# Sums laid along the partitions by one product of ones, with a longer start and a vector load in smaller pieces

## The chip, the cores and the metric

The kernel runs on one core of a Trainium2 chip. Its metric is the device time of one execution in microseconds (us); the time before is the median of 3 runs, 627.53 us.

## The reference

It is one layer of a hybrid encoder: 512 tokens of 2048 features, all in float32. Attention heads and a linear recurrence work side by side on one shared input projection, and one output projection joins them.

```python
h = rms_norm(x, norm_w)                       # (1, 512, 2048)
proj = einsum('bsd,de->bse', h, w_in)         # 4608 columns
q, k, v, g_attn, xr, g_lru = split(proj, ...) # 1024, 256, 256, 1024, 1024, 1024
attn_out = attention_group(q, k, v, ...)      # 8 heads of 128, 2 of k and v; RMS norm of
                                              # q and k per head, axial rope, full softmax
lru_out = lru_group(xr, conv_w, conv_b, ...)  # depthwise convolution of 4 taps, then a gated
                                              # linear recurrence forward and one backward
mixed = concatenate([rms_norm(attn_out, attn_norm_w) * silu(g_attn),
                     rms_norm(lru_out, lru_norm_w) * silu(g_lru)])
return x + einsum('bse,ed->bsd', mixed, w_out)
```

rms_norm divides each token's vector by the root of the mean of its squares. There are three such norms over whole vectors of features: of x, of lru_out and of attn_out. The change touches how the three sums reach the other partitions.

## The kernel before, in words

The layout is mostly features on the 128 partitions and the 512 tokens along the columns. A float32 product is split: each operand becomes a high part in fp32r and a low part (the rest, in fp32r too), and mm3 adds three matmuls in PSUM, high by high, high by low, low by high (L153 to L155). The high part of a weight tile is a cast on ScalarE (L218, wh from the raw weights wr), the low part a subtraction on VectorE (L219, wl). A weight transfer brings 256 input features by 512 columns; a projection takes 8 of them. The output projection is done in 2x2 blocks with seven products in place of eight (L1029).

The order on TensorE is the order of the code throughout, under manual_schedule. On SP, the queue of most transfers, it is written by hand in the start and in the attention, on ScalarE and VectorE in the start and at the end. Elsewhere a scheduler orders the instructions of VectorE, ScalarE and GpSimd, and brings marked ones forward (high_priority). Chains of small work (the recurrence, the norms, the attention) are woven into projections: the chain yields a number, and so many steps of the projection are issued before it goes on.

The parts that the change touches stand in this order in the program:

- **The start.** GpSimd sets constants: ident (an identity, L159), ones (L161), ones_r (a copy of ones in fp32r), nhalf. TensorE begins with WARM = 11 products of ones, the fillers of busy() (L1156), while the first chunk of x and nw_st (the norm's gains) are on their way. Then columns() transposes nw_st (L189), xturn() transposes the first x (L253), ScalarE writes its high part, WARM2 = 5 more fillers run, and the first projection begins (L388).
- **vec_load() (L170)** fetches seven kinds of small vectors (convolution taps conv_w, biases, decay parameters, norm gains) into vec_st, a row of 128 numbers each, in seven transfers on SP's queue. columns(vec, vec_st) then transposes it on TensorE (L189), and the copy (L191) makes vec, in which each vector is a column.
- **rows() (L352)** takes rstd, the 1/rms of x, in which a token is a partition, and has to lay it along the columns, the same on all partitions, as rbc. It splits rstd into a high and a low part, multiplies each with the identity (L360: a diagonal block for each 128 tokens), and adds two products of ones with these diagonals in one PSUM bank (L367). rbc scales the evacuation of each projection (L471).
- **halved() and spread() (L817, L825)** serve the other two norms. The squares are added over the tiles into sums["l"] (hsum, L568 on VectorE and L570 on GpSimd) and sums["a"] (asum, L751 on GpSimd), a column for each token, with 128 partial sums down the partitions. halved() makes a high and a low part of the sum (L821, L822), spread() two products of ones with them (L829), which add up the partitions and leave the total on each, then the square root and the reciprocal, into gbc. kv() calls them for the recurrence beside the attention's q projection, later() for the attention beside the last gate projection.

The calls that a reader needs beside the functions below:

```python
    busy(WARM)
...
        if (c, e) == (4, 2):
            with tc.high_priority(AHEAD):
                vec_load()
        if (c, e) == (7, 1):
            columns(vec, vec_st)
        if (c, e) in ((4, 3), (KT // 2 - 1, 0)):
            with tc.high_priority(AHEAD), tc.issue_after(split_done[-1][1]):
                next(stats)
```

Of the kernel before, what the change touches and what calls it, by code (L numbers as in the profile page):

```python
# [12 lines left out]
F32R = mybir.dt.float32r  # L13
# [4 lines left out]
P = 128  # L18
# [3 lines left out]
NT = SEQ // P  # L22
# [4 lines left out]
NB = 8  # L27
# [12 lines left out]
SOON = 150  # L40


WARM, WARM2 = 11, 5


BEGIN, STEPS, LATE = 11, 2, 3
# [13 lines left out]
R_CW, R_CB, R_BA, R_BX, R_LAM, R_AN, R_LN, R_END = 0, 32, 40, 56, 72, 88, 96, 104  # L60
# [3 lines left out]
def hybrid_kernel(  # L64
# [20 lines left out]
    nc = tc.nc  # L85
# [32 lines left out]
    def nm(s):  # L118
        cnt[0] += 1
        return f"{s}_{cnt[0]}"  # L120
# [22 lines left out]
    def mm():  # L143
        return ps.tile([P, SEQ], F32, tag="mm", name=nm("mm"))

    def const(shape, name, dt=F32):
        return cp.tile(list(shape), dt, tag=name, name=name)

    def f(ap):
        return ap.bitcast(F32)  # L150
# [4 lines left out]
        nc.tensor.matmul(acc, ll, rh, start=False, stop=stop)  # L155


    ident = const([P, P], "ident")
    make_identity(nc, ident)  # L159
    ones = const([P, P], "ones")  # L160
    nc.gpsimd.memset(ones, 1.0)  # L161
    ones_r = const([P, P], "ones_r", F32R)
    nc.gpsimd.memset(f(ones_r), 1.0)
    nhalf = const([P, 48], "nhalf")
    nc.gpsimd.memset(nhalf, -0.5)

    nw_st = const([KT, P], "nw_st")
    vec_st = const([R_END, P], "vec_st")

    def vec_load():  # L170
        for lo, src in (
            (R_CW, conv_w.rearrange("t o (n p) -> (t o n) p", p=P)),
            (R_CB, conv_b.rearrange("(n p) -> n p", p=P)),
            (R_BA, lru_ba.rearrange("d (n p) -> (d n) p", p=P)),
            (R_BX, lru_bx.rearrange("d (n p) -> (d n) p", p=P)),
            (R_LAM, lru_lambda.rearrange("d (n p) -> (d n) p", p=P)),
            (R_AN, attn_norm_w.rearrange("(n p) -> n p", p=P)),
            (R_LN, lru_norm_w.rearrange("(n p) -> n p", p=P)),
        ):
            nc.sync.dma_start(vec_st[lo : lo + src.shape[0], :], src)  # L180
# [62 lines left out]
    def behind(those):  # L243
        stack = ExitStack()
        for ins in those:
            stack.enter_context(tc.issue_after(ins))
        return stack
# [103 lines left out]

    def rows(dst, col, dg):  # L352

        shape = [P, NT, P]
        part = [const([P, NT], nm("part")) for _ in range(2)]
        parts = [dg() for _ in part]
        nc.vector.tensor_copy(part[0].bitcast(F32R), col)
        nc.vector.tensor_sub(part[1], col, part[0])
        for c, d in zip(part, parts):
            nc.vector.tensor_mul(  # L360
                d, ident[:, None, :].broadcast_to(shape), c[:, :, None].broadcast_to(shape)
            )
        yield
        pb = mm()
        for k, d in enumerate(parts):
            d = d.rearrange("p t q -> p (t q)")
            nc.tensor.matmul(pb, ones_r, d, start=k == 0, stop=k == 1)  # L367
        nc.vector.tensor_copy(dst, pb)
        yield

    def xstats():
        s = const([P, NT], "xsum")
        nc.vector.reduce_sum(s, ssq, axis=AX.X)
        rsqrt_mean(rstd, s, DM, NT)
        yield from rows(rbc, rstd, lambda: k2(F32R, (P, NT, P)))
# [278 lines left out]
    def kv(es):  # L654
        turned_k = sent(norm_rope(es, NKV, rk), NKV)
        yield 20
        opened("wx", "right")
        for t in range(NT):
            vv = es[t][:, NKV * HD :]
            vt = pools["qkv"].tile([P, 2, NKV * HD], F32R, tag="v", bufs=NT, name=nm("v"))  # L660
            vh[t], vl[t] = vt[:, 0, :], vt[:, 1, :]
            nc.scalar.copy(vh[t], vv)
            nc.vector.tensor_sub(vl[t], vv, f(vh[t]))
        yield from lru_squares()
        yield 2
        drain(turned_k)
        yield 6
        pair = landed(asides.pop(0))
        for h in range(NKV):
            yield (12, 4)[h]  # L670
            kt = pools["qkv"].tile([P, 2, SEQ], F32R, tag="kt", bufs=NKV, name=nm("kt"))
            kth[h], ktl[h] = kt[:, 0, :], kt[:, 1, :]
            those = split_head(pair, h, kth[h], ktl[h])
        parts = halved(
            sums["l"],
            lambda: pools["rope"].tile([P, SEQ], F32R, tag="kv", bufs=NT, name=nm("kv")),
            those,
        )
        yield 4
        spread(gbc, parts, NB * P)  # L680
# [135 lines left out]

    def halved(src, tile_of, those=()):  # L817

        hi, lo = tile_of(), tile_of()
        with behind(those):  # L820
            nc.scalar.copy(hi, src)  # L821
            nc.vector.tensor_sub(lo, src, f(hi))  # L822
        return hi, lo

    def spread(dst, parts, n, those=()):  # L825

        pb = mm()
        for k, part in enumerate(parts):
            nc.tensor.matmul(pb, ones_r, part, start=k == 0, stop=k == 1)  # L829
        nc.scalar.activation(dst, pb, AF.Sqrt, scale=1.0 / n, bias=eps[:, :1])  # L830
        for t in range(NT):
            ts_ = slice(t * P, (t + 1) * P)
            with behind(those):
                nc.vector.reciprocal(dst[:, ts_], dst[:, ts_])
# [122 lines left out]
    own = []  # L957
# [254 lines left out]
    for step in proj_feat(C_XR, a1, first, given):  # L1212
        if step is None:
            with tc.high_priority():
                first.append(wsplit(raw, 1, nc.vector.tensor_copy))
                xturn(xc, 1)
            xsquare(xc, 0)
            move(None)
            given[1] = wload(w_in, 2 * P, C_XR)
            continue  # L1220
        c, e = step
        move(step)
        if (c, e) == (1, 2):
            s2.close()
# [8 lines that stand above are left out]
# [121 lines left out]
    def later():  # L1354
        with tc.high_priority():
            parts = halved(sums["a"], lambda: fin_s(dt=F32R))
        yield 2
        with tc.high_priority():
            spread(gbc, parts, NH * HD, split_done[turn_of[0] - 2][1:])
        yield 4  # L1360
        for pair in ap_[:2]:
            normed(pair)
        yield 4
        todo = gate(late, ap_[:2], R_AN, fin_s)
        for _ in range(3):
            yield next(todo)
        build(4, ap_[0], [hring.tile([P, 7, H], F32R, name=nm(t)) for t in ("mh", "ml")])
        yield from todo
        for pair in ap_[2:]:
            normed(pair)  # L1370
# [78 lines left out]
```

## Time and profile before

| what | value |
|---|---|
| median of 3 runs | 627.53 us (627.31 to 627.67) |
| span of the profiled execution | 625.3 us (the page gives no other time of that execution) |
| TensorE busy | 620.3 us, 99% of the span, 2758 matmuls |
| TensorE weight loads (beside the matmuls) | 512.8 us, 82% |
| VectorE busy | 494.8 us, 79% |
| ScalarE busy | 353.2 us, 56% |
| GpSimd busy | 101.7 us, 16% |
| DMA | 127.61 MB, mean 204 GB/s |

The profile comes from one execution, and its span runs from the first to the last recorded instruction. In its rows, PE is TensorE, PEld its weight loads, DVE VectorE, ACT ScalarE, POOL GpSimd, SP the engine whose queue issues most transfers; SPq and the like are the queues. L360 is line 360 of the kernel before, and "k<-ident,part" reads: tile k written from ident and part, buffer numbers left out. A matmul's "busy" time overlaps the next one's, so the pace of TensorE is read from the distance of starts, not from its busy share or from the mean of one.

### The profile page before, as it was taken

The numbers are of one execution on the slowest core, as the hardware profiler recorded it, in microseconds if no ns is written. First come the engines' busy times: TensorE is split into PE (matmuls) and PEld (weight loads), VectorE is DVE, ScalarE is ACT, GpSimd is POOL, SyncE is SP. The second block draws the span as 40 slices with busy tenths as digits, with TensorE's granted clock in tenths as the row PEclk, the third lists the DMA queues.
The fourth block names the chain that finished last, engine by engine and source line by source line (L and its number), as shares of the span: only waits on it lengthen the run. The fifth ranks groups of instructions, "written<-read, shape, count | busy, mean of one in ns | idle before, by whom it ended". The sixth has DMA issues, their size and how long they took to land.

```text
span 625.3 us, 8281 instructions
## 1 busy us (share of the span) xinstructions
PE 620.3 (99%) x2758; PEld 512.8 (82%) x2758; DVE 494.8 (79%) x796; ACT 353.2 (56%) x617; POOL 101.7 (16%) x134
## 2 busy tenths in 40 slices
PE   9999999999999999999999999999999999999997
PEld 7888888888888888888888888888888888888886
DVE  5967979986699875987887888549979866886886
ACT  3764899479945823545485448428445633443441
POOL 0000210112003531622123223100310101010010
PEclk9999999999999999999999999999999999999999
DMA  8878785859774599479658646923995677896262
GB/s 289 293 210 253 179 206 163 175 136 197 236 231 140 169 235 250 103 204 273 186 175 258 201 140 192 265 79 106 261 248 185 210 253 240 293 327 233 68 202 101
DMA packets 73595, 127.61 MB, mean 204 GB/s; under 512 B 6617, under 2 KB 29265, under 8 KB 73553
## 3 DMA queue, kind: packets, MB, share of 16 engines
q1 hardware_dynamic: 65664, 109.65, 56.7%
q0 software_dynamic: 7712, 17.31, 14.3%
q8 instruction: 21, 0.34, 0.2%
q14 instruction: 22, 0.17, 0.1%
q10 hardware_dynamic: 176, 0.14, 0.1%
HBM read 110.29 MB, written 37.75 MB: 237 GB/s over the span
## 4 chain that ended last, share of the span: by engine, by line
PE 99%; DVE 0%; issue 0%; POOL 0%; POOLq 0%
PE pj L153 20%; PE pj L154 20%; PE pj L155 20%; PE mm L1029 14%; PE pj L1029 11%; PE mm L155 3%; PE mm L154 3%; PE mm L153 3%; PE pj L388 2%; PE mm L253 1%; PE mm L1156 1%; PE mm L829 0%; PE mm L367 0%; DVE cb L1058 0%; PE mm L189 0%
## 5 line engine op out<-in xcount | busy, mean ns | idle before, releaser
L153 PE MATMUL pj<-x,wh 128*128 128x512 f32 x368 | 143.5, 390 | 0.0
L155 PE MATMUL pj<-x,wl 128*128 128x512 f32 x368 | 143.2, 389 | 0.0
L154 PE MATMUL pj<-x,wh 128*128 128x512 f32 x368 | 143.2, 389 | 0.0
L218 ACT CAST wh<-wr 128x512 fp32r<-128x512 f32 x142 | 84.9, 620 | 78.9 <-PE pj L154 31.2
L219 DVE TENSOR_TENSOR wl<-wr,wh 128x512 fp32r<-128x512 f32 x144 | 99.9, 724 | 19.7 <-ACT wh L218 18.6
L881 ACT CAST wh<-wr 128x1024 fp32r<-128x1024 f32 (+1 forms) x72 | 60.8, 862 | 75.7 <-PE mm L1029 34.6
L882 DVE TENSOR_TENSOR wl<-wr,wh 128x1024 fp32r<-128x1024 f32 (+1 forms) x72 | 68.8, 985 | 30.5 <-ACT wh L881 30.3
L155 PEld LDWEIGHTS pj<-x,wl 128*128 128x128 f32 x368 | 69.1, 188 | 14.5
L153 PEld LDWEIGHTS pj<-x,wh 128*128 128x128 f32 x368 | 69.1, 188 | 14.3
L154 PEld LDWEIGHTS pj<-x,wh 128*128 128x128 f32 x368 | 69.1, 188 | 14.3
L153 PE MATMUL pj<-wh,x 128*128 128x512 f32 x192 | 74.7, 389 | 0.0
L155 PE MATMUL pj<-wh,x 128*128 128x512 f32 x192 | 74.7, 389 | 0.0
L154 PE MATMUL pj<-wl,x 128*128 128x512 f32 x192 | 74.7, 389 | 0.0
L905 POOL DMA_DIRECT2D t<-in_w_out_dram x40 | 33.5, 891 | 156.6 <-DMA t<-in_w_out_dram 99.4
L1029 PE MATMUL mm<-wh,ml 128*128 128x512 f32 x126 | 49.0, 389 | 0.0
L1029 PE MATMUL mm<-wh,mh 128*128 128x512 f32 x126 | 49.0, 389 | 0.0
L1029 PE MATMUL mm<-wl,mh 128*128 128x512 f32 x126 | 49.0, 389 | 0.0
L155 PEld LDWEIGHTS pj<-wh,x 128*128 128x128 f32 x192 | 36.0, 188 | 7.6
L153 PEld LDWEIGHTS pj<-wh,x 128*128 128x128 f32 x192 | 36.0, 188 | 7.5
L154 PEld LDWEIGHTS pj<-wl,x 128*128 128x128 f32 x192 | 36.0, 188 | 7.4
L706 POOL TENSOR_SCALAR p<-p,sm 128x512 f32<-128x512 f32 x32 | 24.3, 762 | 89.4 <-DVE sm L705 89.4
L1029 PE MATMUL pj<-wl,mh 128*128 128x512 f32 (+1 forms) x100 | 38.5, 385 | 0.0
(201 smaller groups left out, 1053.6 us busy)
## 6 DMA issues: line engine op xcount, KB each, us to landing
wr<-in_w_in_dram SPq DMA_DIRECT2D x71, 512.0 KB, 5.1
wr<-in_w_out_dram SPq DMA_DIRECT2D x24, 512.0 KB, 5.1
t<-in_w_out_dram POOLq DMA_DIRECT2D x40, 256.0 KB, 6.9
wr<-t SPq DMA_DIRECT2D x40, 256.0 KB, 5.4
pd<-u SPq DMA_DIRECT2D x16, 512.0 KB, 3.0
pt<-pd SPq DMA_DIRECT2D x64, 128.0 KB, 3.6
t<-in_w_out_dram SPq DMA_DIRECT2D x24, 256.0 KB, 5.4
t<-t SPq DMA_DIRECT2D x16, 256.0 KB, 5.1
```

Source lines behind the costliest of these rows:

```text
L153: nc.tensor.matmul(acc, lh, rh, start=start, stop=False)
L154: nc.tensor.matmul(acc, lh, rl, start=False, stop=False)
L155: nc.tensor.matmul(acc, ll, rh, start=False, stop=stop)
L218: copy(hi, raw[:, k, :]).ins,
L219: nc.vector.tensor_sub(lo, raw[:, k, :], f(hi)).ins,
L253: nc.tensor.transpose(pt[:, t * P : (t + 1) * P], xc[:, t, ks], ident)
L388: nc.tensor.matmul(acc[e], w[:, e * P : (e + 1) * P], x_[2 * c + k], start=c == k == j == 0, stop=False,)
L706: last_pool[0] = nc.gpsimd.tensor_scalar(p, p, sm, 0.0, op0=ALU.mult, op1=ALU.add).ins
L881: nc.scalar.copy(hi[:, to], b)
L882: nc.vector.tensor_sub(lo[:, to], b, f(hi[:, to]))
L905: nc.gpsimd.dma_start(dst, src, accum_op=ALU.add)
L1029: nc.tensor.matmul(dst[s][:, es], lh[:, ts_], rh[:, es], start=i == ends_[0] and j == 0, stop=i == ends_[1] and j == 2,)
```

## The change

Four edits:

- **One product.** rows() puts the high part of a token's value into one half of the partitions and the low part into the other half: "two" holds both, and both_ is a matrix that carries the 64x64 identity in each of its four quarters, so that each column of the operand d has two nonzero entries, the high part and the low part. One product of ones adds them. halved() first adds the upper 64 partitions of the sum to the lower 64 (on VectorE, in place), then writes the high part of those 64 into the lower half of one tile and the low part into the upper half; spread() does one product.
- **The constants.** VectorE sets ones, as its first instruction, and GpSimd has one memset less; GpSimd makes both_ from ident with an addition and a copy, after ident and nhalf.
- **The fillers.** WARM is 12 in place of 11.
- **The loads.** vec_load() fetches the four convolution taps in four transfers of 8 rows each in place of one of 32 rows.

```diff
--- before.py
+++ after.py
@@ -40,7 +40,7 @@
 SOON = 150
 
 
-WARM, WARM2 = 11, 5
+WARM, WARM2 = 12, 5
 
 
 BEGIN, STEPS, LATE = 11, 2, 3
@@ -155,21 +155,29 @@
         nc.tensor.matmul(acc, ll, rh, start=False, stop=stop)
 
 
+    ones = const([P, P], "ones")
+    nc.vector.memset(ones, 1.0)
     ident = const([P, P], "ident")
     make_identity(nc, ident)
-    ones = const([P, P], "ones")
-    nc.gpsimd.memset(ones, 1.0)
     ones_r = const([P, P], "ones_r", F32R)
     nc.gpsimd.memset(f(ones_r), 1.0)
     nhalf = const([P, 48], "nhalf")
     nc.gpsimd.memset(nhalf, -0.5)
 
+    both_ = const([P, P], "both")
+    half = P // 2
+    nc.gpsimd.tensor_add(both_[:, :half], ident[:, :half], ident[:, half:])
+    nc.gpsimd.tensor_copy(both_[:, half:], both_[:, :half])
+
     nw_st = const([KT, P], "nw_st")
     vec_st = const([R_END, P], "vec_st")
 
     def vec_load():
         for lo, src in (
-            (R_CW, conv_w.rearrange("t o (n p) -> (t o n) p", p=P)),
+            *(
+                (R_CW + t * NB, conv_w[t].rearrange("o (n p) -> (o n) p", p=P))
+                for t in range(R_CB // NB)
+            ),
             (R_CB, conv_b.rearrange("(n p) -> n p", p=P)),
             (R_BA, lru_ba.rearrange("d (n p) -> (d n) p", p=P)),
             (R_BX, lru_bx.rearrange("d (n p) -> (d n) p", p=P)),
@@ -351,20 +359,21 @@
 
     def rows(dst, col, dg):
 
-        shape = [P, NT, P]
-        part = [const([P, NT], nm("part")) for _ in range(2)]
-        parts = [dg() for _ in part]
-        nc.vector.tensor_copy(part[0].bitcast(F32R), col)
-        nc.vector.tensor_sub(part[1], col, part[0])
-        for c, d in zip(part, parts):
-            nc.vector.tensor_mul(
-                d, ident[:, None, :].broadcast_to(shape), c[:, :, None].broadcast_to(shape)
-            )
+        shape = [P, NT, 2, P // 2]
+        two = const([P, NT, 2], "two", F32R)
+        for n in range(2):
+            own, other = (slice(m * P // 2, (m + 1) * P // 2) for m in (n, 1 - n))
+            nc.vector.tensor_copy(two[own, :, n], col[own])
+            nc.vector.tensor_sub(two[other, :, n], col[own], f(two[own, :, n]))
+        d = dg()
+        nc.vector.tensor_mul(
+            d.rearrange("p t (h q) -> p t h q", h=2),
+            both_.rearrange("p (h q) -> p h q", h=2)[:, None].broadcast_to(shape),
+            f(two)[:, :, :, None].broadcast_to(shape),
+        )
         yield
         pb = mm()
-        for k, d in enumerate(parts):
-            d = d.rearrange("p t q -> p (t q)")
-            nc.tensor.matmul(pb, ones_r, d, start=k == 0, stop=k == 1)
+        nc.tensor.matmul(pb, ones_r, d.rearrange("p t q -> p (t q)"), start=True, stop=True)
         nc.vector.tensor_copy(dst, pb)
         yield
 
@@ -816,17 +825,18 @@
 
     def halved(src, tile_of, those=()):
 
-        hi, lo = tile_of(), tile_of()
+        both = tile_of()
+        low, high = src[: P // 2], src[P // 2 :]
+        nc.vector.tensor_add(low, low, high)
         with behind(those):
-            nc.scalar.copy(hi, src)
-            nc.vector.tensor_sub(lo, src, f(hi))
-        return hi, lo
-
-    def spread(dst, parts, n, those=()):
+            nc.scalar.copy(both[: P // 2], low)
+            nc.vector.tensor_sub(both[P // 2 :], low, f(both[: P // 2]))
+        return both
+
+    def spread(dst, both, n, those=()):
 
         pb = mm()
-        for k, part in enumerate(parts):
-            nc.tensor.matmul(pb, ones_r, part, start=k == 0, stop=k == 1)
+        nc.tensor.matmul(pb, ones_r, both, start=True, stop=True)
         nc.scalar.activation(dst, pb, AF.Sqrt, scale=1.0 / n, bias=eps[:, :1])
         for t in range(NT):
             ts_ = slice(t * P, (t + 1) * P)
```

The lines after rows() are 9 further down in the changed kernel's own numbering (L471 is L480 there, L568 is L577), and L219 is L227, L180 is L188. Where the scheduler sets the order, it comes out in another way at some places. Three of them follow.

On VectorE near 50 us of the profile, where the first projection ends: rbc is copied, vec is copied, the first banks are evacuated (ev), and the low parts wl of the next projection's weights are made. Before:

```order
L368 COPY rbc<-mm_626 128x512
L219 TENSOR_TENSOR wl_737<-wr_734,wh_736 128x512
L219 TENSOR_TENSOR wl_741<-wr_734,wh_740 128x512
L500 TENSOR_TENSOR k_121_705<-k_112_684,k_120_704 128x512
L191 COPY vec<-mm_636 128x104
L471 TENSOR_TENSOR ev_696<-pj_161,rbc 128x512
L471 TENSOR_TENSOR ev_698<-pj_162,rbc 128x512
L471 TENSOR_TENSOR ev_700<-pj_163,rbc 128x512
```

Now:

```order
L377 COPY rbc<-mm_632 128x512
L480 TENSOR_TENSOR ev_701<-pj_165,rbc 128x512
L480 TENSOR_TENSOR ev_703<-pj_166,rbc 128x512
L199 COPY vec<-mm_641 128x104
L227 TENSOR_TENSOR wl_742<-wr_739,wh_741 128x512
L227 TENSOR_TENSOR wl_746<-wr_739,wh_745 128x512
L480 TENSOR_TENSOR ev_705<-pj_167,rbc 128x512
L509 TENSOR_TENSOR k_118_710<-k_109_689,k_117_709 128x512
```

Two evacuations and the copy of vec moved ahead of the two low parts.

On SP's queue, near the end of the first projection, stand the loads of the small vectors and behind them the weights of the next projection (wr) and the recurrence's gate maps (k). Before:

```order
L180 DMA vec_st<-in_conv_w_dram 32x128
L180 DMA vec_st<-in_conv_b_dram 8x128
L180 DMA vec_st<-in_lru_ba_dram 16x128
L180 DMA vec_st<-in_lru_bx_dram 16x128
L180 DMA vec_st<-in_lru_lambda_dram 16x128
L180 DMA vec_st<-in_attn_norm_w_dram 8x128
L180 DMA vec_st<-in_lru_norm_w_dram 8x128
L206 DMA wr_734<-in_w_in_dram 128x2x512
```

Now four loads of conv_w stand in place of the first row, and everything behind them is three places further back; the prediction shows the rows.

On VectorE near 205 us, in kv(), where the recurrence's squares are added up and the sum is handed to halved(). Before:

```order
L281 STREAM_TRANSPOSE uq_2057<-kv_1680 128x2x4x32
L568 TENSOR_TENSOR hsum<-hsum,hsq_2039 128x1024
L219 TENSOR_TENSOR wl_2273<-wr_2270,wh_2272 128x512
L219 TENSOR_TENSOR wl_2277<-wr_2270,wh_2276 128x512
L613 TENSOR_TENSOR ev_2100<-ev_2100,rr_2108 128x512
```

The rows of now are in the prediction: the addition of the two halves (64x512) stands between L568 and the two low parts, and so a wait for GpSimd's L570 does too.

## The prediction

> **What bounds the kernel now.** I read the page's first section, then TensorE's waits, then its chain, then the chip's time in three stretches.
>
> ```profile
> span 625.3 us, 8281 instructions
> PE 620.3 (99%) x2758; PEld 512.8 (82%) x2758; DVE 494.8 (79%) x796; ACT 353.2 (56%) x617; POOL 101.7 (16%) x134
> PE mm L1156 <- POOL ones L161: 1.1, 1, 1.1
> 5.70:621.40 615.70, 615.70 (x2739) 1.00 0.72 205
> ...
> 621.40:625.30 3.90, 0.03 (x1) 0.00 (x0) 0.42 (x1) 0.00 (x0) 0.00 (x0) 0.81 0.40 134
> ```
>
> A busy share of 99% alone would not prove a bound, since matmuls overlap. But the only wait that the list of TensorE's waits shows is the first 1.1 us, for the tile of ones. From 5.70 to 621.40 it is busy for all 615.70 us, and the last 3.90 us are the end of the output. The chain of waits says how fast it goes in between; its columns are start, duration, what.
>
> ```profile
> 1.13 2.53 PE mm L1156 x11
> 3.66 0.21 PE mm L189
> 3.87 1.05 PE mm L253 x4
> 4.92 1.07 PE mm L1156 x5
> 5.98 1.02 PE pj L388 x4
> 7.00 0.44 PE mm L253 x4
> 7.44 3.20 PE pj L388 x14
> ...
> 49.70 0.46 PE mm L367 x2
> ...
> 236.69 0.46 PE mm L829 x2
> ...
> 427.74 0.46 PE mm L829 x2
> ```
>
> Matmuls of 512 columns follow each other every 0.23 us (3.20 / 14), and the products with ones, L367 and L829, go at just that pace: 0.46 us a pair. So the time is the start (6 us), TensorE's list of matmuls at 0.23 us, and the tail. A matmul fewer is worth 0.23 us for certain, unless it opens a wait; a change on another engine is worth nothing until it makes TensorE wait.
>
> The page gives the span of 625.3 us and no time of that execution; the median of the runs, 627.53, is 2.2 us more, and I take those 2.2 us as unchanged. What one run can differ by is seen in 627.31 to 627.67.
>
> **One product of ones in place of two.** Three pairs become single products: 3 x 0.46 / 2 = 0.69 us off TensorE's list. That is the largest term. What replaces them lies on VectorE, ScalarE and GpSimd, and must be ready in time:
>
> ```profile
> L360 DVE TENSOR_TENSOR k<-ident,part x2: 683/684/684, 36.5 to 37.1; 128x512 fp32r<-128x512 f32 x2
> L357 DVE CAST part<-rstd x1: 171/171/171, 36.3 to 36.3; 128x4 fp32r<-128x4 f32 x1
> L568 DVE TENSOR_TENSOR hsum<-hsum,hsq x3: 1186/1187/1222, 198.8 to 204.0; 128x1024 f32<-128x1024 f32 x3
> L570 POOL TENSOR_TENSOR hsum<-hsum x1: 1621/1621/1621, 205.3 to 205.3; 128x512 f32<-128x512 f32 x1
> L822 DVE TENSOR_TENSOR kv<-hsum,kv x1: 693/693/693, 227.2 to 227.2; 128x512 fp32r<-128x512 f32 x1
> L751 POOL TENSOR_TENSOR asum<-asum,p x7: 1289/1295/1822, 322.6 to 420.0; 128x512 f32<-128x512 f32 x7
> L822 DVE TENSOR_TENSOR s<-asum,s x1: 676/676/676, 422.4 to 422.4; 128x512 fp32r<-128x512 f32 x1
> ```
>
> In rows(), one multiplication of 0.68 us goes and two small instructions come (0.17 each, as L357): the operand is ready at about 37.5 instead of 37.8, and TensorE takes it at 49.7. Nothing there. In halved(), an addition of 64x512 comes ahead of the cast. Its nearest row is L822's 0.69 us (as many columns, half the partitions; below it lies nothing cheaper of that width). The first halved() has its parts at 227.9, and they are read at 236.7: 8.8 us of cover. The second has them at 422.4 + 0.68 = 423.1, read at 427.7: 4.6 us of cover against 0.7, and against about 1.7 more for two casts of hs that ScalarE now does ahead. Cost 0; if the cover were gone, the cost would be what exceeds it.
>
> The first new addition waits on GpSimd's L570, and it stands right behind the last L568 in VectorE's queue:
>
> ```order
> L577 TENSOR_TENSOR hsum<-hsum,hsq_2044 128x1024
> L830 TENSOR_TENSOR hsum<-hsum 64x512
> L227 TENSOR_TENSOR wl_2278<-wr_2275,wh_2277 128x512
> L227 TENSOR_TENSOR wl_2282<-wr_2275,wh_2281 128x512
> L622 TENSOR_TENSOR ev_2105<-ev_2105,rr_2113 128x512
> ```
>
> So VectorE stands still from 205.2 to 206.9, and the two low parts wl of weights behind it come later. What the same stretch holds today:
>
> ```profile
> 205.07 2.39 DVE L219 TENSOR_TENSOR wl<-wr,wh 128x512 fp32r<-128x512 f32 x2
> 209.07 0.69 DVE L613 TENSOR_TENSOR ev<-ev,rr 128x512 f32<-128x512 f32 x1 [1.62 <-POOL rr L347]
> ...
> 216.68 1.29 DVE L219 TENSOR_TENSOR wl<-wr,wh 128x512 fp32r<-128x512 f32 x2
> ```
>
> The pair took 2.39 us beside GpSimd's L570 and takes 1.29 without it. New: addition 206.9 to 207.6, pair to 208.9, and then L613, which waits for GpSimd until 209.07 anyway. The stall of 1.7 us fits into the gap of 1.62 us and the faster pair. Cost 0.
>
> **Ones set by VectorE, and a twelfth filler.** The fillers L1156 multiply the ones while the first x is on its way.
>
> ```profile
> 0.72 0.20 POOL masks.py:197 MEMSET ident<- 128x128 f32 x1 [0.29 <-POOLq L1434]
> 0.86 0.21 POOL L161 MEMSET ones<- 128x128 f32 x1
> L191 DVE COPY nw<-mm x1: 175/175/175, 3.9 to 3.9; 128x16 f32<-128x16 f32 x1
> 52.60 0.26 DVE L191 COPY vec<-mm 128x104 f32<-128x104 f32 x1
> ```
>
> Today ones end at 1.07 and TensorE begins at 1.13. No row shows VectorE's memset; between its copies of 16 and of 104 columns it is 0.17 to 0.26 us, from 0.72 as the other engines: ones at 0.89 to 0.98, TensorE at 0.95 to 1.04, that is 0.09 to 0.18 earlier. A filler costs 1.07 / 5 = 0.21. So the fillers end 0.03 to 0.12 later, and L189, the transposes L253, ScalarE's x and the first L388 follow. I take +0.07. The lower bound is 0 (the transposes would wait for x's transfer anyway), the upper one +0.33 (the memset starts only after GpSimd's, 0.93, takes 0.26: TensorE at 1.25, and the filler on top).
>
> The pair above is the row for that upper bound: VectorE and GpSimd slow each other when both work on SBUF. The Trainium skill, "SBUF — State Buffer", section "Who interferes with whom", says that one of the two fully blocks while the other holds a shared port pair, for some of VectorE's kinds of instruction; the trace agrees for L219 (2.39 against 1.29), and no run here shows a memset. [...]
>
> GpSimd's two added instructions make both_ by 2.5 us or so, and it is read at 37.
>
> **Taps one by one.** One transfer becomes four on SP's queue, ahead of the weights of the next product:
>
> ```order
> L188 DMA vec_st<-in_conv_w_dram 8x128 x4
> L188 DMA vec_st<-in_conv_b_dram 8x128
> L188 DMA vec_st<-in_lru_ba_dram 16x128
> L188 DMA vec_st<-in_lru_bx_dram 16x128
> L188 DMA vec_st<-in_lru_lambda_dram 16x128
> L188 DMA vec_st<-in_attn_norm_w_dram 8x128
> L188 DMA vec_st<-in_lru_norm_w_dram 8x128
> L214 DMA wr_739<-in_w_in_dram 128x2x512
> ```
>
> Behind vec_st's loads, three issues more: the weights wr and the gate maps move back.
>
> ```profile
> 41.93 0.32 SPq L180 DMA_DIRECT2D vec_st<-in_attn_norm_w_dram  x1
> 42.59 0.28 SPq L180 DMA_DIRECT2D vec_st<-in_lru_norm_w_dram  x1
> 42.97 0.40 SPq L206 DMA_DIRECT2D wr<-in_w_in_dram  x1
> DMA to landing us min/median/max: 2.1/3.6/5.5
> 47.47 1.30 ACT L218 CAST wh<-wr 128x512 fp32r<-128x512 f32 x2 [1.06 <-PE pj L154]
> 50.80 1.28 DVE L219 TENSOR_TENSOR wl<-wr,wh 128x512 fp32r<-128x512 f32 x2
> 54.26 0.39 PE L153 MATMUL pj<-x,wh 128*128 128x512 f32 x1
> 51.38 0.25 PE L189 MATMUL mm<-ident,vec_st 104*128 104x104 f32 x1
> ```
>
> Each issue takes 0.3 to 0.4 us: +1.0 us or so. The high parts of wr are then ready at 49.8 and read at 54.3. The low parts wait for VectorE, which now puts two evacuations ahead of them, +1.2 us: ready at about 53.3, read at 54.7. The last of vec_st has landed by 42.6 + 5.5 = 48.1 at the latest, by 49.1 with the change, and the transpose L189 reads it at 51.4. Cost 0 in all three, with 1.4 us as the smallest cover.
>
> Sum: 625.3 - 0.69 + 0.07 = 624.7 for the span, 627.53 - 0.62 = 626.9 us for the median.
>
> **Rivals.** (a) The saving is given back: TensorE, 0.23 to 0.69 us ahead, meets producers that do not move with it. For it: VectorE is 79% busy. Against it: the list of waits has nothing for TensorE after 1.1 us, and the producers' own waits are mostly for TensorE, so that they come forward too. Price: the 0.69, 627.5 to 627.9 with the start's upper bound.
>
> (b) The array reaches its full pace sooner. In the chain 256-column fillers need 0.21 and four L388 1.02, where later four need 0.91; the transposes need 1.05 a four and later 0.44. Were all of it at full pace, 0.11 + 0.61 = 0.72 us would go: 626.1 to 626.8. For it: TensorE begins 0.1 us earlier and idles less. Against it: what follows the transposes waits for ScalarE and for weights. The Trainium skill, "TensorE: Matmul & The Clock Gate", Part 1, says that a free-running window of about 3.4 us decides; by that rule an earlier start moves the mean by only a part of the 0.1 us, and one look cannot show it.
>
> (c) The end on the other side: the taps' loads do not overlap. If each of the three waits for the landing of another (2.1 to 5.5 us), vec_st is complete 6.3 to 16.5 us later, up to 48.1 + 16.5 = 64.6, and TensorE stands at L189 from 51.4 on. It decides from 3.3 us of delay, turns the whole slower at 3.9, and is over 0.2% at 5.2: with 8 us it is 627.5 - 0.6 + 4.7 = 631.6. Against it: seven issues went out within 5.4 us while each took 2.1 to 5.5 us to land, so they do overlap.
>
> **How the numbers follow.** 0.2% is 1.25 us, about what a measurement of this kernel can tell from no change. The forecast (626.8 to 627.2 by the start's bounds) has 0.68, (a) 0.14, (b) 0.08, (c) 0.05; 0.05 is left for waits at other places, since the scheduler also reordered VectorE's and ScalarE's work from 50 to 75 and from 420 to 460 us. All but (c), the far end of (b) and that rest lie within 0.2%: faster 0.07, same 0.86, slower 0.07. The range is 626.2 to 627.9: from (b) to (a) with the start's upper bound.
>
> **What would show it.** TensorE with 2756 matmuls, one product each at the lines of the pairs, first start at 0.95 to 1.04, first L388 product between 0 and 0.33 later, no new wait in its list, and a span of 624.6 to 625.0. I am wrong if TensorE's list of waits has an entry beyond its start, above all near 51, 207 or 425 us, or if the first product is more than 0.33 us away from where it is.

## The result, and the profile after

The changed kernel takes 632.29 us (median of 4 runs, 631.73 to 633.39) against 627.42 (4 runs, 627.22 to 627.67): the ratio is 1.0079, 95% interval 1.0065 to 1.0092. It is slower by 4.9 us, where 626.9 was forecast. The profiled execution has a span of 631.2 us. From its page:

```profile
span 631.2 us, 8286 instructions
PE 626.3 (99%) x2756; PEld 512.9 (81%) x2756; DVE 496.3 (79%) x800; ACT 352.4 (56%) x617; POOL 101.7 (16%) x135
```

TensorE has the 2756 matmuls that were forecast and is busy for 6 us more. Its waits (line waited for, us in total, times, longest; behind halved() the changed kernel's lines are 10 further down, not 9, so that L1166 is L1156 of the kernel before):

```profile
PE mm L1166 <- DVE ones L159: 1.0, 1, 1.0
PE pj L155 <- DVE wl L227: 0.2, 1, 0.2
```

So hardly a microsecond of the 5.9 is a wait. The rest has to be the matmuls themselves, and busy time doesn't tell how many fit into a stretch. The table by stretch does: its columns are the stretch, its length and TensorE's busy time in it with the number of matmuls, the granted clock, the DMA share and GB/s. First the kernel before, then the changed one:

```profile
100.00:190.00 90.00, 90.00 (x399) 1.00 0.73 188
190.00:265.00 75.00, 75.00 (x332) 1.00 0.72 183
270.00:420.00 150.00, 150.00 (x663) 1.00 0.68 200
432.00:465.00 33.00, 33.00 (x147) 1.00 0.92 230
470.00:615.00 145.00, 145.00 (x641) 1.00 0.65 214
```

```profile
100.00:190.00 90.00, 90.00 (x397) 1.00 0.72 187
190.00:265.00 75.00, 75.00 (x327) 1.00 0.69 174
270.00:420.00 150.00, 150.00 (x658) 1.00 0.70 203
432.00:465.00 33.00, 33.00 (x147) 1.00 0.83 214
470.00:615.00 145.00, 145.00 (x630) 1.00 0.68 221
```

Every stretch is busy throughout and the granted clock is 1.00, but in 470 to 615 us 630 matmuls are done where 641 were: 230 ns for one instead of 226. From 190 to 265 five are missing, from 432 to 465 none. From start to start, nearly all matmuls of 512 columns of the kernel before are 226 or 227 ns apart. In the changed kernel some 1030 are 229 ns or more apart, most of them 230 to 236; before there are some 75. Summed over all distances below 245 ns, the excess over 226.7 ns is 5.95 us, against 0.35 before. That is +5.6 of the +5.9.

What do the slow ones have in common? Not the engines beside them: from 191 to 254 us they are slow whether VectorE, ScalarE and the DMAs are busy or not (the mean distance is 231.5 ns while VectorE is busy and 230.8 while it is idle). What they have in common is the places of their operands. The constants are laid out one behind the other, and the tiles of the left side (raw weights, x, weights of the projections, later the output's operands) begin behind them. both_ added 512 bytes in each partition. rows() now has one tile "two" of 32 bytes; before it had two tiles "part" of 16 bytes, each rounded up to 32. So everything on the left moved by 512 - 32 = 480 bytes. The tiles of the right side (the recurrence's, q, k, v, the attention's, the first half of the output's operands) stayed. Starts in a partition, modulo 256 bytes, as the program allocates them:

```
kernel            left tiles   right tiles
before               192          192
changed              160          192
```

The slow matmuls stand where one of the operands is from the left and the other from the right (456 matmuls, which lose 2.8 us), or next to a change from one pair of places to another. There they lose 3.1 us although their own two operands are at equal places, all of it in the last matmul before such a change and the next eight behind it. The 1140 that are equal and farther away lose nothing.

From 191 to 254 us the weights of the q projection lie in buffers of the left (xw) and of the right side (wx) in turn, beside x on the left; from 432 to 465 all operands are on the left, and nothing is slow.

What else there is, the chain of the changed kernel shows. Its start:

```profile
1.04 2.74 PE mm L1166 x12
3.79 0.21 PE mm L197
4.00 1.05 PE mm L261 x4
5.04 1.07 PE mm L1166 x5
6.11 1.41 PE pj L397 x4
7.52 0.44 PE mm L261 x4
```

The first product L397 begins at 6.11 instead of 5.98: +0.13, as forecast (between 0 and 0.33). These four need 1.41 instead of 1.02, because TensorE comes to its full pace later in this execution: the first three start distances are 593, 426 and 285 ns, in the kernel before 456, 224 and 231. And at 43 us:

```profile
34.61 3.82 DMA xu<-xd
38.44 3.93 DMA vec_st<-in_conv_w_dram
42.37 0.58 DVE x L347
...
43.59 0.69 DVE wl L227
44.32 0.50 PE pj L155
```

Rows of x that travel through DRAM (xu) come late, ScalarE's and VectorE's work on them does too, the low part wl behind it in VectorE's queue as well, and TensorE's starts are 0.84 us further apart in all around here. Sum: 5.6 + 0.5 + 0.8 - 0.7 for the three products = 6.2 us on TensorE; the tail behind its last matmul is 0.3 shorter.

This execution took 633.39 us, the longest of the four and 1.1 us above their median. The median's +4.9 is just the 5.6 of the pace less the 0.7 of the products. So most of the start's 0.5 and the 0.8 at 43 us are probably this execution's own; there is no second profile of the changed kernel that could show it.

### The profile page after: what moved, and what is told of

Same layout as the page of the kernel before. It is cut to its first block, busy times and chain, and to the rows that moved or that the text cites. A ratio compares the mean times of both kernels' runs of the same rounds, so it can differ in the third digit from the quotient of the medians.

```text
span 631.2 us, 8286 instructions
## 1 busy us (share of the span) xinstructions
PE 626.3 (99%) x2756; PEld 512.9 (81%) x2756; DVE 496.3 (79%) x800; ACT 352.4 (56%) x617; POOL 101.7 (16%) x135
## 4 chain that ended last, share of the span: by engine, by line
PE 96%; DMA 2%; DVE 1%; issue 0%; SPq 0%
PE pj L155 19%; PE pj L153 19%; PE pj L154 19%; PE mm L1039 14%; PE pj L1039 11%; PE mm L155 4%; PE mm L153 3%; PE mm L154 3%; PE pj L397 2%; DMA xd<-xu 1%; PE mm L261 1%; DMA vec_st<-in_conv_w_dram 1%; DMA xu<-xd 1%; PE mm L1166 1%; DVE wl L227 0%; DVE x L269 0%
## 5 line engine op out<-in xcount | busy, mean ns | idle before, releaser
L227 DVE TENSOR_TENSOR wl<-wr,wh 128x512 fp32r<-128x512 f32 x144 | 98.7, 713 | 21.5 <-ACT wh L226 20.4
L1039 PE MATMUL pj<-wh,mh 128*128 128x512 f32 (+1 forms) x100 | 39.0, 390 | 0.0
L1039 PE MATMUL pj<-wh,ml 128*128 128x512 f32 (+1 forms) x100 | 38.9, 389 | 0.0
```

Of the source, the lines that this page charges most:

```text
L227: nc.vector.tensor_sub(lo, raw[:, k, :], f(hi)).ins,
L1039: nc.tensor.matmul(dst[s][:, es], lh[:, ts_], rh[:, es], start=i == ends_[0] and j == 0, stop=i == ends_[1] and j == 2,)
```

## The experiments

Theory 1: TensorE is slowed where the two operands that it reads at once, moving data and weights, start at different places modulo some power of two (64 bytes, I thought at first). Theory 2: the moved instructions, loads and waits make it slow. The first seven kernels move tiles and nothing else; each engine's instructions keep the order that they have in the kernel that was edited. An unused tile of so many bytes behind the constants does it for the left side:

```diff
     nc.gpsimd.memset(eps, EPS)
+    const([P, 8], "gap")           # 8 x 4 = 32 bytes; 16 and 32 for 64 and 128 bytes
```

**The changed kernel, left tiles back to 192.**

> The changed kernel with 32 unused bytes a partition allocated behind its constants, the order of the instructions unchanged. In its profile TensorE's matmuls of 512 columns start 226.7 ns apart where both operands lie at the same offset in 64 bytes, and some 233 ns apart where one tile starts at a multiple of 64 bytes and the other 32 bytes behind one; the slow ones add up to 5.8 us. The constants became 480 bytes longer (512 for both_, less 32 for one tile 'two' in place of two of 'part'), so all tiles of the left side moved by 32 modulo 64. Theory 1 (offset between the operands): the pad takes the offset away; 626.5 to 627.5 us. Theory 2 (the moved instructions, waits and loads make it slow): 631.5 to 633 us, as without the pad.

Measured: 626.77 us (11 runs, 626.14 to 627.66), against 627.29 for the kernel before on the same chip; ratio 0.9991 (0.9982 to 1.0000). 32 unused bytes take away 5.5 us, and what is left is the forecast's time, 626.9, to 0.1. The same stretches of its profile:

```profile
190.00:265.00 75.00, 75.00 (x333) 1.00 0.73 184
...
470.00:615.00 145.00, 145.00 (x641) 1.00 0.64 212
```

The 641 are back, with all instructions in the changed order. Theory 2 falls.

**The kernel before, left tiles at 224.**

> The kernel before with 32 unused bytes behind its constants and nothing else: all tiles of the left side move by 32 bytes. Theory 1: slower by the 5 to 6 us of the slow matmuls, 632 to 633.5 us, and the profile shows 230 to 236 ns between matmuls whose operands differ by 32 modulo 64. Theory 2: 627.2 to 627.7 us, no change.

Measured: 634.36 us (4 runs), ratio 1.0110 (1.0097 to 1.0124). Nothing of the change is in this kernel, and it is slower than the changed one, and than theory 1's 632 to 633.5 us; some 1155 matmuls are 229 ns or more apart, with an excess of 7.3 us. As many as in the changed kernel (456) have operands at different places, and they lose 3.1 us; the equal ones next to a change lose 4.1 instead of 3.1, and why it is more here stays open.

**The kernel before, left tiles at 0.**

> The kernel before with 64 unused bytes behind its constants: all tiles of the left side move by a multiple of 64. Theory 1: 627.2 to 627.7 us, no change. Theory 3 (any shift of the left tiles against the right ones costs, the kernel before had a lucky layout): 630 us or more.

Measured: 631.69 us (5 runs), ratio 1.0070 (1.0058 to 1.0083), where theory 1 expected no change. The period of 64 bytes that I had read from the changed kernel is wrong. A period of 128 or 256 bytes, or theory 3, remained: left and right are equal modulo 256 in the kernel before (192 and 192) and differ by 64 here.

**The changed kernel, right tiles moved by 32 too: 160 and 160.** The unused tile that the kernel keeps on the right grows from 32 to 64 bytes.

```diff
-    opened("pad", "right").tile([P, 8], F32, name="pad")
+    opened("pad", "right").tile([P, 16], F32, name="pad")
```

> The changed kernel with the tiles of the right side moved by 32 bytes as well, so that nearly all operands, left and right, start 32 bytes behind a multiple of 64. Theory 1 (the difference between the two operands counts): 626.5 to 627.5 us, all matmuls 226.7 ns apart. Theory 1b (a start that is no multiple of 64 costs by itself): slower than the changed kernel, 633 us or more. Theory 2: 631.5 to 633 us.

Measured: 626.58 us (11 runs, 626.08 to 627.83), ratio 0.9993 (0.9984 to 1.0002). No tile of the large products stands at a multiple of 64, and nothing is slow. So a start that is no multiple of 64 costs nothing by itself; the difference between the operands does. The place of the left side is not at fault either: 160 there is slow beside 192 on the right and fast beside 160.

**The kernel before, left tiles at 64.**

> The kernel before with 128 unused bytes behind its constants. 32 bytes made it 634.4 us and 64 bytes 631.7, so the offset that counts is not one within 64 bytes. Tiles of the left and the right side stood at the same place modulo 256 in all fast kernels so far. Theory 1 with a period of 128 bytes: 627.0 to 627.7 us and matmuls 226.7 ns apart. Theory 1 with a period of 256 bytes: 630 us or more.

Measured: 631.80 us (4 runs), ratio 1.0071 (1.0057 to 1.0084). The period is not 128 either.

**The kernel before, x alone moved by 32 bytes.** In the projections the weights then stand at 192 and x at 224.

```diff
         lo = pool.tile([P, SEQ], F32R, tag="wl", bufs=4, name=nm("wl"))
+        if not split_done:
+            pool.tile([P, 8], F32, tag="gap", bufs=1, name="gap")
```

> The kernel before with 32 unused bytes ahead of the tiles of x (x2) alone: in the projections, 1680 matmuls, the two operands then lie 32 bytes apart, throughout and without any change from matmul to matmul; the recurrence, the attention and the output projection keep their places. Theory 1 (the distance between the two operands that TensorE reads at once counts): some 6 to 7 ns for each of the 1680, 10 to 11.5 us more, 637 to 639 us. Theory 1c (only a change of offset from one matmul to the next costs): below 630 us, the slow matmuls stand only where a projection meets other work.

Measured: 638.72 us (4 runs, 638.59 to 638.93), ratio 1.0180 (1.0165 to 1.0196): 11.45 us more, as theory 1 had it. By the program there are 36 x 16 x 3 = 1728 such matmuls, not 1680; at 6.6 ns each they make 11.4 us. The stretches of its profile:

```profile
190.00:265.00 75.00, 75.00 (x323) 1.00 0.66 177
...
432.00:465.00 33.00, 33.00 (x143) 1.00 0.71 193
470.00:615.00 145.00, 145.00 (x639) 1.00 0.68 220
```

Now the stretch from 432 to 465, which was whole in the changed kernel, loses 4 matmuls of 147, and the output projection is nearly whole (the projections end at 480 us here). The lines of one product tell the same; the first fence is of the kernel before, the second of this one (ns of one, shortest, median, longest):

```profile
L155 PE MATMUL pj<-x,wl x368: 388/389/398, 20.5 to 468.6; 128*128 128x512 f32 x184
L155 PE MATMUL pj<-wh,x x192: 388/389/395, 109.1 to 250.4; 128*128 128x512 f32 x192
```

```profile
L155 PE MATMUL pj<-x,wl x368: 392/396/400, 20.5 to 480.1; 128*128 128x512 f32 x184
L155 PE MATMUL pj<-wh,x x192: 387/396/397, 111.4 to 256.5; 128*128 128x512 f32 x192
```

It makes no difference which operand moves and which is loaded: in the first row x moves and the weight tile is loaded, in the second the weight tile moves and x is loaded, and both medians go from 389 to 396.

**The kernel before, x alone moved by 256 bytes.** The same edit with more elements:

```diff
+            pool.tile([P, 64], F32, tag="gap", bufs=1, name="gap")
```

> The kernel before with 256 unused bytes ahead of the tiles of x (x2) alone, where 32 bytes made it 638.7 us. Theory 1 with a period of 256 bytes: 627.0 to 627.6 us, as the kernel before. Theory 4 (it is the gap itself or the moved tiles, not the place modulo 256): 630 us or more.

Measured: 627.43 us (10 runs), ratio 1.0003 (0.9994 to 1.0012). The gap and the move cost nothing; the place modulo 256 does.

Over all profiles, the mean distance of starts where the pair of places (moving operand, weights, modulo 256) stays the same for eight matmuls before and eight behind; how many there are stands in brackets, and the few distances that hold a wait are left out:

```
equal:      192,192  226.7 (2561, before)    160,160  226.7 (2560, after_right32)
            64,64    226.8 (860, pad128)     0,0      226.8 (863, pad64)
            224,224  226.7 (862, before_pad32)
different:  224,192  233.3 (540, x2gap32)    192,224  233.3 (480, x2gap32)
            160,192  233.3 (112, changed)    64,192   233.3 (112, pad128)
            0,192    229.1 (112, pad64)
```

Differences of 32 and of 128 bytes cost 6.6 ns a matmul, one of 64 (moving at 0, weights at 192) cost 2.4. The other way round (moving at 192, weights at 0), which stands in shorter runs alone, it was 233.3 ns too (18 matmuls with five of the same pair ahead and one behind). Where the pair changes, the matmul ahead and the next few, up to eight, are slow as well, the equal ones among them; that is why the recurrence and the attention, whose own operands are all on the right, lose time too.

Then the parts of the change, without the moved tiles.

**The single product alone.** Changed are rows(), halved(), spread() and both_, with 32 unused bytes; ones, fillers and taps as before. Of the change's diff these lines are undone, and the tile is added:

```diff
-WARM, WARM2 = 12, 5
+WARM, WARM2 = 11, 5
-    nc.vector.memset(ones, 1.0)
+    nc.gpsimd.memset(ones, 1.0)          # behind make_identity, as before
-                (R_CW + t * NB, conv_w[t].rearrange("o (n p) -> (o n) p", p=P))
+            (R_CW, conv_w.rearrange("t o (n p) -> (t o n) p", p=P)),
+    const([P, 8], "gap")
```

> The kernel before with the single product of ones in rows(), halved() and spread() alone (ones, fillers and taps as before), and 32 unused bytes that put the left tiles back to their place modulo 256. The prediction's sum: three matmuls fewer, 0.68 us less than the kernel before. Rival (the saving is given back, TensorE meets producers): no change, within 0.2 us.

Measured: 626.65 us (11 runs, 626.33 to 627.62), ratio 0.9990 (0.9981 to 0.9999): 0.62 us less, the prediction's 0.69 within what these runs resolve. The interval, 0.06 to 1.2 us less, would allow the rival's 0.2 as well; the profile speaks against it, with a span of 624.6 instead of 625.3 and no new wait of TensorE:

```profile
PE mm L1163 <- POOL ones L161: 1.1, 1, 1.1
```

**The taps one by one alone.** In the kernel before:

```diff
-            (R_CW, conv_w.rearrange("t o (n p) -> (t o n) p", p=P)),
+            *(
+                (R_CW + t * NB, conv_w[t].rearrange("o (n p) -> (o n) p", p=P))
+                for t in range(R_CB // NB)
+            ),
```

> The kernel before with the four convolution taps fetched one by one and nothing else; no tile moves. The prediction: no change, within 0.2 us of the kernel before. Rival (the three more issues on SP's queue delay the rows of x or the next weights): the waits of TensorE near 43 us that the changed kernel shows, 0.8 us more than the kernel before.

Measured: 627.25 us against 627.27 (11 runs), ratio 0.9999 (0.9990 to 1.0008). They cost nothing that can be measured, and the wait at 43 us is not in its profile. The scheduler's order on ScalarE and VectorE changes with this edit too.

**Ones by VectorE and the twelfth filler alone.** In the kernel before:

```diff
-WARM, WARM2 = 11, 5
+WARM, WARM2 = 12, 5
-    nc.gpsimd.memset(ones, 1.0)
+    nc.vector.memset(ones, 1.0)          # ahead of ident
```

> The kernel before with ones set by VectorE and 12 fillers in place of 11, and nothing else; no tile beside ones and ident changes its place. The prediction's term: 0.07 us more, between 0 and 0.33. Rival (the array is at full pace sooner, by 0.72 us at most): faster by 0.2 us or more.

Measured: 627.13 us against 627.27 (11 runs), ratio 1.0003 (0.9994 to 1.0012). The median is a little lower and the ratio a little above 1: neither the 0.07 more nor a gain can be told from nothing.

**The changed kernel with left tiles back and 11 fillers.** In the changed kernel:

```diff
-WARM, WARM2 = 12, 5
+WARM, WARM2 = 11, 5
...
+    const([P, 8], "gap")
```

> The changed kernel with the 32 bytes that put the left tiles back, and 11 fillers as before. By the prediction's sum: 0.69 us for the products and 0.09 to 0.18 us for the earlier ones, 626.4 to 626.5 us; that is 0.2 us below the one with 12 fillers (626.8). Rival (the fillers only fill the wait for x): as with 12, 626.6 to 626.9 us.

Measured: 626.94 us (11 runs, 626.43 to 627.24), ratio 0.9993 (0.9984 to 1.0002), against 626.77 with 12. That is just above the rival's 626.6 to 626.9 and well above the sum's 626.4 to 626.5: a filler less brings nothing that can be measured. Of all kernels here, only the one with the single product and the 32 bytes alone has an interval that lies below 1 as a whole.

## Why the prediction was wrong

**The step that failed** is the sentence on both_: "GpSimd's two added instructions make both_ by 2.5 us or so, and it is read at 37." It prices the new tile's instructions and leaves out its bytes. In the same way, "two small instructions come" in rows() leaves out that two tiles of constants became one. 512 bytes more and 32 less put every left tile 480 bytes further, 32 bytes off its old place modulo 256, and this costs 5.5 us (632.29 against 626.77). No rival named it, and the 0.05 for "waits at other places" looked for waits, where the loss is in the pace of matmuls that never wait. The list of waits, in which the prediction would have looked for its error, has one new entry of 0.2 us, at 43 us; only the span, 631.2 instead of 624.6 to 625.0, gave it away.

**"TensorE's list of matmuls at 0.23 us" as a constant** failed with it. The pace was read from a kernel in which all large tiles stood at 192 modulo 256; it is 0.2267 us there and 0.2333 where the operands' places differ by 32 bytes. "A matmul fewer is worth 0.23 us for certain" agrees with single_only (0.62 us for three), but the price of all the others had been taken as given.

**The sum was right where the tiles stay:** 626.9 forecast, 626.77 measured with the pad. The runs resolve the sum, but not its small terms. Rival (a), the saving given back, did not show: with the single product alone 0.62 of the 0.69 us stay.

**halved() and its stall.** Forecast: a stall of 1.7 us, then the addition, then the pair of wl's at its faster pace, no cost. From the timeline of the changed kernel on VectorE (start, length, what, and in brackets the idle time ahead and what ended it):

```profile
207.72 0.69 DVE L830 TENSOR_TENSOR hsum<-hsum 64x512 f32<-64x512 f32 x1 [1.47 <-POOL hsum L579]
208.50 1.29 DVE L227 TENSOR_TENSOR wl<-wr,wh 128x512 fp32r<-128x512 f32 x2
210.70 0.69 DVE L622 TENSOR_TENSOR ev<-ev,rr 128x512 f32<-128x512 f32 x1 [0.91 <-POOL rr L355]
```

The stall is 1.47 us, the addition 0.69, the pair 1.29 as it is without GpSimd beside it, and VectorE then waits for GpSimd anyway. Right. In later(), the addition of asum starts at 425.5 and takes 0.69, the two parts are done at 428.7, and their product starts at 431.2: 2.5 us of cover are left, where the forecast's 4.6 less 0.7 and 1.7 made 2.2. Right too.

**Ones and fillers.** From the timeline of the changed kernel:

```profile
0.82 0.17 DVE L159 MEMSET ones<- 128x128 f32 x1 [0.82 <-PEq L1444]
```

VectorE's memset took 0.165 us (0.17 to 0.26 forecast) although GpSimd's memsets of ident and ones_r ran beside it, from 0.72 to 1.07. So it was not slowed as the pair of L219 was, and what the upper bound stood on did not come about. It started at 0.82, though, and not at 0.72 as assumed; late start and short memset cancel, and TensorE began at 1.04, the late end of 0.95 to 1.04. First L397 +0.13, in the range; its worth is below what the runs can tell.

**Taps.** Right at no cost (taps_only), and rival (c) did not happen. But the delay on SP's queue is larger than the 1.0 us of the forecast. In the changed kernel's timeline:

```profile
37.97 4.83 SPq L188 DMA_DIRECT2D vec_st<-in_conv_w_dram  x4
...
44.88 0.29 SPq L188 DMA_DIRECT2D vec_st<-in_lru_norm_w_dram  x1
```

The last load is issued at 44.88 instead of 42.59, 2.3 us later. The cover held.

**Rival (b)**, the array at full pace sooner, is real but has nothing to do with the change. In the profile with the 32 bytes, whose span is 624.0:

```profile
1.04 2.74 PE mm L1166 x12
3.78 0.20 PE mm L197
3.98 0.60 PE mm L261 x4
...
5.36 1.19 PE pj L397 x4
```

The four transposes need 0.60 instead of 1.05, and the span is 0.7 us below the forecast's 624.7, as the rival had it; but this execution is the fastest of its 11 (626.14 us against the median of 626.77). Over the 13 profiles, the distances of starts drop between 2.7 and 6.1 us behind the first filler (512 columns from 427 ns to 227, 256 columns from 213 to 109). Kernels with 11 fillers have 3.3 as well as 6.1, those with 12 fillers 2.7 as well as 5.9. The Trainium skill, "TensorE: Matmul & The Clock Gate", Part 1, says that the window is free-running, so that the moment depends on where in it the first matmul falls; the trace agrees with that, over a wider spread (3.4 us in all) than the half microsecond to either side that it names.

**Open** is the wait near 43 us. It stands in three of the 13 profiles: in the changed kernel (0.84 us) and in the kernels before with 32 and with 128 unused bytes (0.42 and 0.49), each of them with left and right tiles at different places. Two further kernels of that kind don't have it, nor any with equal places. In all three, ScalarE gets its rows of x through DRAM at 39.6 us or later. The chain at 43 us also passes through a load of the taps; but the other two kernels with the wait fetch the taps in one transfer, and taps_only doesn't have it. Whether the places of the tiles delay these rows, or chance does, no run here tells; the taps alone don't.

## What to carry to other kernels

A new constant, or one of another size, moves every tile that is allocated behind it. Where TensorE is the bound, compare the starts of its operands modulo 256 before and after an edit, as far as they are like the ones here (fp32r, 512 columns, a weight load for each matmul); an unused tile of the missing bytes puts them back, and on the right or the left is the same. And when a kernel gets slower without a wait, count the matmuls in equal stretches of both profiles: a busy share of 99% reads the same at 226.7 and at 233.3 ns.

## What the runs showed of the hardware

- TensorE reads two operands that both start at the same place modulo 256 bytes at 226.7 ns for 512 columns of fp32r with a weight load each, whatever that place is (0, 64, 160, 192 and 224 were seen). With a difference of 32 or 128 bytes it is 233.3 ns; for 32 bytes it makes no difference which operand is ahead. For 64 bytes it was 229.1 with the moving operand at 0 and the weights at 192, and 233.3 the other way round. Other differences were not run.
- The Trainium skill, "SBUF — State Buffer", section "A bandwidth-pool intuition that's wrong (but worth ruling out)", gives TensorE a second, independent read port for the loading of weights. The trace does not agree with full independence: a matmul takes up to 6.6 ns more, depending on where its two operands start relative to each other, here and in the matmuls just before and behind. That the two reads get in each other's way is the likely reading; where in the chip they would meet, no run here shows.
- TensorE's matmuls come to full pace 2.7 to 6.1 us behind the first one, differently in each of the 13 profiles, whether 11 or 12 fillers stand ahead. The first four products took 1.02 us in one profile and 1.41 in another; so differences of half a microsecond at the start can't be read from one profile each.
